# Seven Strassen products in place of the direct w1 and w3 products of a two-layer trunk, and w2 by groups of four blocks between them

## The chip, the core and the metric

One core of one Trainium2 chip runs the whole program in one launch. The metric is device time in microseconds, the median of several executions. The core has five engines: TensorE (PE; its weight loads are listed apart as PEld), VectorE (DVE), ScalarE (ACT), GpSimd (POOL) and SyncE (SP), which here issues the DMAs. Each works through a queue of its own in order and waits on semaphores for the others.

## The reference, cut to what matters

A sequence of 512 tokens with 1024 features goes through two layers. Each has a mixer (layer 0 sparse attention and pooling, layer 1 stick-breaking attention) and then a gated feed-forward part; both add to the residual x. All is float32, and the hidden width of the feed-forward part is 2816, that is 22 blocks of 128.

```python
def swiglu(h, w1, w3, w2):
    return (jax.nn.silu(h @ w1) * (h @ w3)) @ w2

for layer in range(DEPTH):
    ...
    h = rms_norm(x, norm_ffn_g[layer])
    x = x + swiglu(h, ffn_w1[layer], ffn_w3[layer], ffn_w2[layer])
```

## The kernel before, in words

The residual stands transposed: eight tiles xs of 128 features by 512 tokens. Every product of two float32 matrices is made of three passes: each operand is split into a high part, rounded to float32r, and the low rest, and TensorE adds high x high, high x low and low x high into one PSUM bank (`prods`, lines 204 to 206). A weight piece of 128x1024 is loaded by SP into a `raw` tile (three buffers), ScalarE writes the high part wh (`copy`, line 176), VectorE subtracts to get the low part wl (`split`, line 187). There are three pairs of wh and wl.

`Norm.chunk(c)` makes the two parts hh and hl of x times gain for one chunk of features (lines 253, 254) and adds its square to acc (264, 265). The factor of the norm, rb, comes from acc later (`stats`, `bcast`) and is multiplied in after the product.

`ffn(layer, nrm, nxt)` first loops over the 22 blocks f. For each it loads and splits the piece of w1 and of w3 and does 24 matmuls of 128x512 for each (8 chunks of features, three passes). Then it takes a = p1*rb on VectorE (308), silu on ScalarE (310), s*rb on GpSimd (311), a = p3*s on VectorE (312), and splits a into gh and gl (317 on ScalarE, 318 on VectorE). After all 22 blocks a second loop runs over the eight output chunks n: three pieces of w2, 66 matmuls of 128x512 into one bank, one addition to x (331), and then either the next layer's `chunk(n)` or the store to out.

The program is put to a scheduler in the order of the code. It assigns buffers and writes one fixed order for each engine. The mixers are written as steps in two tables, EVEN_ORDER and ODD_ORDER; their last steps, `oa` and `x` with first argument 1, are the output projections, which end with `nxt.chunk(n)`, so that the feed-forward part begins while they run.

## Time and profile before

| what | value |
|---|---|
| median of 3 runs | 1203.85 us (1203.02 to 1203.98) |
| span of the profiled execution, first to last instruction | 1202.7 us |
| TensorE busy | 1177.3 us, 98% |
| VectorE, ScalarE, GpSimd busy | 621.2, 481.0, 294.2 us |
| mean granted TensorE clock | 0.993 |
| DMA | 102.36 MB, mean 85 GB/s |

The page gives the profiled execution by its span alone; the median of the runs is 1.15 us longer. Matmuls are pipelined: the time of one in a row (some 0.39 us for 128x512) is its way through the array, and what a matmul costs in a stream is the distance from its start to the next one's. By the timeline, the even mixer lasts to 202.7 us, layer 0's w1/w3 loop to 444.0 us, its w2 loop to some 565 us, then the odd mixer to some 838 us, layer 1's w1/w3 loop to 1077.4 us and its w2 loop to the end.

### The profile page before, as it was taken

What the parts mean: (1) busy time and instruction counts of PE and PEld (TensorE: products, weight loads), DVE (VectorE), ACT (ScalarE), POOL (GpSimd) and SP (SyncE); (2) the same over time, 40 slices, a digit from 0 to 9 for tenths busy, and PEclk for the clock granted to TensorE, in tenths of its full rate; (3) what the DMA queues carried; (4) which work ended last, traced back from release to release, by engine and by line L of the source; (5) the groups of instructions that cost most, each with busy time, mean ns of one, the idle gap of its engine ahead of it and who ended that gap; (6) DMA issues with size and microseconds to landing.
All of it is one profiled execution on the core that took longest, in us unless ns stands there. A gap on an engine that the chain in (4) does not pass through costs nothing. (4 is left out here: it accounts for less than half of the span.)

```text
span 1202.7 us, 13889 instructions
## 1 busy us (share of the span) xinstructions
PE 1177.3 (98%) x5415; PEld 967.4 (80%) x5416; DVE 621.2 (52%) x851; ACT 481.0 (40%) x704; POOL 294.2 (24%) x324
## 2 busy tenths in 40 slices
PE   6999999999999999999999999999999999999998
PEld 3886758888888888888888888888888888888887
DVE  7499956434443433333457878867444434432221
ACT  4354564322223222223248778865323232321110
POOL 5246644111111110001023445433211111110000
PEclk8999999999999999999999999999999999999999
DMA  5222102232323223333221111112323233333330
GB/s 186 83 70 75 40 32 70 88 105 90 104 90 103 91 93 97 97 96 105 88 88 53 53 36 53 54 53 70 105 90 103 90 103 95 99 96 114 112 112 22
DMA packets 30737, 102.36 MB, mean 85 GB/s; under 512 B 3792, under 2 KB 4304, under 8 KB 30672
## 3 DMA queue, kind: packets, MB, share of 16 engines
q1 hardware_dynamic: 30240, 101.46, 26.4%
q8 instruction: 42, 0.69, 0.2%
q14 instruction: 23, 0.19, 0.1%
q10 hardware_dynamic: 432, 0.02, 0.0%
HBM read 99.37 MB, written 2.10 MB: 84 GB/s over the span
## 5 line engine op out<-in xcount | busy, mean ns | idle before, releaser
L205 PE MATMUL psum<-hl,wh_ffn_w 128*128 128x512 f32 x704 | 274.0, 389 | 0.3 <-DVE hl L254 0.3
L206 PE MATMUL psum<-hh,wl_ffn_w 128*128 128x512 f32 x704 | 274.1, 389 | 0.0
L204 PE MATMUL psum<-hh,wh_ffn_w 128*128 128x512 f32 x704 | 273.7, 389 | 0.0
L176 ACT ACTIVATE wh_ffn_w<-raw_ffn_w 128x1024 fp32r<-128x1024 f32 x88 | 93.4, 1061 | 305.4 <-PE psum L205 305.4
L311 POOL TENSOR_TENSOR s<-s,rb 128x512 f32<-128x512 f32 x44 | 76.8, 1748 | 378.3 <-ACT s L310 378.3
L205 PEld LDWEIGHTS psum<-hl,wh_ffn_w 128*128 128x128 f32 x704 | 132.2, 188 | 28.3 <-DVE hl L254 0.7
L206 PEld LDWEIGHTS psum<-hh,wl_ffn_w 128*128 128x128 f32 x704 | 132.2, 188 | 27.5
L204 PEld LDWEIGHTS psum<-hh,wh_ffn_w 128*128 128x128 f32 x704 | 132.2, 188 | 27.0
L204 PE MATMUL psum<-gh,wh_ffn_w 128*128 128x512 f32 x352 | 138.7, 394 | 0.0
L206 PE MATMUL psum<-gh,wl_ffn_w 128*128 128x512 f32 x352 | 138.0, 392 | 0.0
L205 PE MATMUL psum<-gl,wh_ffn_w 128*128 128x512 f32 x352 | 136.6, 388 | 0.0
L187 DVE TENSOR_TENSOR wl_ffn_w<-raw_ffn_w,wh_ffn_w 128x1024 fp32r<-128x1024 f32 x88 | 109.2, 1240 | 23.2 <-ACT wh_ffn_w L176 22.8
L176 ACT ACTIVATE wh_ffn_w<-raw_w 128x1024 fp32r<-128x1024 f32 (+1 forms) x48 | 47.5, 990 | 183.3 <-PE psum L205 158.5
L187 DVE TENSOR_TENSOR wl_ffn_w<-raw_w,wh_ffn_w 128x1024 fp32r<-128x1024 f32 (+1 forms) x48 | 54.6, 1137 | 122.4 <-ACT wh_ffn_w L176 122.4
L312 DVE TENSOR_TENSOR a<-psum,s 128x512 f32<-128x512 f32 x44 | 30.4, 691 | 138.2 <-PE psum L206 134.7
L308 DVE TENSOR_TENSOR a<-psum,rb 128x512 f32<-128x512 f32 x44 | 30.4, 692 | 107.4 <-PE psum L206 107.3
L206 PEld LDWEIGHTS psum<-gh,wl_ffn_w 128*128 128x128 f32 x352 | 66.1, 188 | 15.5
L205 PEld LDWEIGHTS psum<-gl,wh_ffn_w 128*128 128x128 f32 x352 | 66.1, 188 | 14.8
L204 PEld LDWEIGHTS psum<-gh,wh_ffn_w 128*128 128x128 f32 x352 | 66.2, 188 | 13.2
L265 POOL TENSOR_TENSOR acc<-acc,sq 128x512 f32<-128x512 f32 x28 | 42.0, 1501 | 140.4 <-ACT sq L264 139.7
L254 DVE SCALAR_TENSOR_TENSOR hl<-x,gain_t,hh 128x512 fp32r<-128x512 f32 x32 | 42.0, 1329 | 4.0 <-ACT hh L253 4.0
L204 PE MATMUL psum<-hh,wh_q 128*128 128x512 f32 x96 | 39.0, 406 | 1.8 <-DVE wh_q L178 1.8
(293 smaller groups left out, 2083.2 us busy)
## 6 DMA issues: line engine op xcount, KB each, us to landing
raw_ffn_w<-in_w_dram SPq DMA_DIRECT2D x88, 512.0 KB, 3.5
raw_w<-in_w_dram SPq DMA_DIRECT2D x32, 512.0 KB, 3.5
raw_w<-in_w_dram SPq DMA_DIRECT2D x16, 384.0 KB, 3.1
raw_v<-in_w_v_dram SPq DMA_DIRECT2D x8, 512.0 KB, 3.6
raw_q<-in_w_qk_dram SPq DMA_DIRECT2D x8, 512.0 KB, 3.5
raw_k<-in_w_qk_dram SPq DMA_DIRECT2D x8, 512.0 KB, 3.5
raw_o<-in_w_o_dram SPq DMA_DIRECT2D x8, 512.0 KB, 3.5
x<-in_x_dram SPq DMA_DIRECT2D x8, 256.0 KB, 5.3
```

The lines of the kernel that those rows point to most:

```text
L176: ac.activation(dst, src, AF.Copy, scale=scale)
L187: (ve if lo_eng == "dve" else gp).tensor_sub(lo[:, :cols], raw[:, :cols], f32(hi[:, :cols]))
L204: te.matmul(ps, wh, ah, start=(first and i == 0), stop=False)
L205: te.matmul(ps, wh, al, start=False, stop=False)
L206: te.matmul(ps, wl, ah, start=False, stop=(last and i == n - 1))
L254: ve.scalar_tensor_tensor(lo, xt, g, f32(hi), op0=ALU.mult, op1=ALU.subtract)
L265: gp.tensor_add(self.acc, self.acc, sq)
L308: ve.tensor_mul(a, p1, nrm.rb)
L311: gp.tensor_mul(s, s, nrm.rb)
L312: ve.tensor_mul(a, p3, s)
```

## The change

The first pair of blocks (f = 0, 1 in the old numbering) keeps the direct products (`Plain`, 24 matmuls of 128x512 for each of its four pieces), ordered by chunk of features. From the second pair on, ten pairs for each layer, each pair of blocks of w1 and likewise of w3 becomes a `Job`: the pair's weights are a two by two arrangement (block of the pair by even or odd chunk of features), and the activations are one too (even or odd chunk by half of the tokens). Seven products replace eight. Each is 12 matmuls of 128x256 (four pairs of chunks, three passes), so a Job has 84 of these where 48 of 128x512 stood. Products 1, 6, 7 and 4 add up in one bank A, 5 and 3 in a bank C, and 2 is alone in B. Between them ScalarE copies bank A out (u after product 1, u after 6, v after 7), and the next product adds to the same bank. VectorE puts the halves together (`put`).

Added work: for each layer `sums` makes the four sums T1 to T4 of the activations (8 copies on ScalarE, 16 operations of 128x256 on GpSimd, and four splits). For each Job GpSimd makes four sums of weights (128x512, lines 475 to 478 of the new kernel), and ScalarE and VectorE split the raw first block, the two tiles of sums s12 and s34 (128x1024 each) and the block a22 (128x512).

w2 is done by `Down(q, m)`: four blocks of the hidden dimension (the last group has two) times two output chunks, 24 matmuls of 128x512 into two banks, then two additions to x. One stands after each Job from the third pair on; the rest stand at the end. The number of w2 matmuls is the same, 528 for each layer; additions to x in this part rise from 16 to 88 in all.

Memory moves as well: the pools of a mixer and of the norm's tiles are closed before its output projection, so that the tiles of the feed-forward part can be opened there; its first pieces are loaded during steps 4 and 6 of that projection. The feed-forward part has four raw buffers and five pairs of wh and wl.

```diff
-    def ffn(layer, nrm, nxt):
-        with tc.tile_pool(name=f"ffn{layer}", bufs=1) as fp:
-            gs = []
-            for f in range(NF):
-                wa = weights(w13[layer, f, 0], f"ffn_w1_{layer}_{f}")
-                wb = weights(w13[layer, f, 1], f"ffn_w3_{layer}_{f}")
-                p1 = take()
-                dense(p1, wa, nrm.h)
-                if f == 0:
-                    nrm.stats()
...
-            for n in range(KC):
-                ps = take((n,))
-                pairs = []
-                for k0 in range(0, NF, 8):
...
-                    pairs += [(wcol(w, k - k0), gs[k]) for k in range(k0, k1)]
-                prods(ps, pairs)
-                ve.tensor_add(xs[n], xs[n], ps)
...
+        def sums(self, i, pool):
+            b = pool.tile([P, 4, HT], F32, name=f"b{self.idx}_{i}", tag="s12")
+            t = pool.tile([P, 4, HT], F32, name=f"t{self.idx}_{i}", tag="s34")
+            for e in range(2):
+                c = 2 * i + e
+                dst = b[:, 2 * e : 2 * e + 2, :].rearrange("p a b -> p (a b)")
+                ac.activation(dst, xs[c], AF.Copy, scale=gain_t[:, self.idx, c : c + 1])
+            gp.tensor_sub(t[:, 0, :], b[:, B12, :], b[:, B11, :])
+            gp.tensor_sub(t[:, 1, :], b[:, B22, :], t[:, 0, :])
+            gp.tensor_sub(t[:, 2, :], b[:, B22, :], b[:, B12, :])
+            gp.tensor_sub(t[:, 3, :], b[:, B21, :], t[:, 1, :])
+            hi, lo = self.pairs[i]
+            ac.copy(hi[:, 4:8, :], t)
+            ve.tensor_sub(lo[:, 4:8, :], t, f32(hi[:, 4:8, :]))
...
+            self.nraw += 1
+            return (self.fr if self.nraw % 4 == 1 else rawp).tile([P, D], F32, name=name, tag="raw")
...
+            self.nsplit += 1
+            p = self.fw if self.nsplit % 5 in (1, 2) else wsp
+            return [p.tile([P, D], F32R, name=f"w{x}_{name}", tag=f"w{x}") for x in "hl"]
...
+        def gated(f, i):
+            q, r = divmod(f, 2)
+            if (f, i) == (2 * q, 1) or q not in gsplit:
+                if q not in gsplit:
+                    p = (big, stage.more)[q % 2]
+                    gsplit[q] = [p.tile([P, 4, T], F32R, name=f"gs{x}_{layer}_{q}", tag=f"o{x}") for x in "hl"]
+            h, l = [t[:, 2 * r + i, :] for t in gsplit[q]]
+            src = values[f][i]
+            ac.copy(h, src)
...
+                gp.tensor_add(z[0], a21, a22)
+                gp.tensor_sub(z[1], z[0], a11)
+                gp.tensor_sub(z[2], a11, a21)
+                gp.tensor_sub(z[3], a12, z[1])
+                wa = split_into(stage.two(f"a{name}"), raw[0])
+                w12 = split_into(stage.two(f"s{name}"), s12)
+                w34 = split_into(stage.two(f"t{name}"), s34)
+                h = stage.fr.tile([P, n, P], F32R, name=f"wh_b{name}", tag="wbh")
+                l = stage.fr.tile([P, n, P], F32R, name=f"wl_b{name}", tag="wbl")
+                ac.copy(h, a22)
+                ve.tensor_sub(l, a22, f32(h))
...
+            BANK = {1: "A", 6: "A", 7: "A", 4: "A", 2: "B", 5: "C", 3: "C"}
+            RHS = {1: B11, 2: B21, 3: B22, 4: T4, 5: T1, 6: T2, 7: T3}
+            def prod(self, p):
+                b = self.BANK[p]
+                first = b not in self.open
+                if first:
+                    self.open[b] = take()
+                ps = self.open[b][:, :HT]
+                r = self.RHS[p]
+                for k in range(KC // 2):
+                    wh, wl = self.wt[p](k)
+                    ah, al = (x[:, r, :] for x in nrm.pairs[k])
+                    te.matmul(ps, wh, ah, start=first, stop=False, skip_group_check=True)
+                    te.matmul(ps, wh, al, start=False, stop=False, skip_group_check=True)
+                    te.matmul(ps, wl, ah, start=False, stop=(k == KC // 2 - 1), skip_group_check=True)
+                    first = False
+                nm = f"{self.w}_{layer}_{self.f}"
+                if p == 1:
+                    self.u = stage.fg.tile([P, T], F32, name=f"u{nm}", tag="u")
+                    ac.copy(self.u[:, LAT], ps)
+                elif p == 6:
+                    ac.copy(self.u[:, ERL], ps)
+                elif p == 7:
+                    self.u3 = stage.fr.tile([P, HT], F32, name=f"v{nm}", tag="u3")
+                    ac.copy(self.u3, ps)
+                    self.put(1, ERL, self.u3, "C")
+                elif p == 2:
+                    self.put(0, LAT, self.u[:, LAT], "B")
+                    give(self.open["B"])
+                elif p == 4:
+                    self.put(1, LAT, None, "A")
+                    give(self.open["A"])
+                elif p == 3:
+                    self.put(0, ERL, self.u[:, ERL], "C")
+                    give(self.open["C"])
+            def put(self, i, half, a, b):
+                ps = self.open[b][:, :HT]
+                last = (i, half) in ((1, LAT), (0, ERL))
+                c = gate_tile(self.f)[i]
+                d = c if self.w == 0 else value_tile(self.f)[i]
+                if a is not None:
+                    ve.tensor_add(d[:, half], ps, a)
+                if self.w:
+                    if a is None:
+                        ve.tensor_mul(d[:, half], ps, c[:, half])
+                    elif i == 1:
+                        ve.tensor_mul(d[:, half], d[:, half], c[:, half])
+                    elif last:
+                        ve.tensor_mul(d, d, c)
+                    if last:
+                        gated(self.f, i)
+                elif a is None:
+                    ve.tensor_mul(d[:, half], ps, rb(half))
+                    ve.tensor_mul(d[:, ERL], d[:, ERL], rb(ERL))
+                elif last:
+                    ve.tensor_mul(d, d, nrm.rb)
+                if last and self.w == 0:
+                    ac.activation(d, d, AF.Silu)
+                    gp.tensor_mul(d, d, nrm.rb)
...
+        class Down:
...
+                self.ps = [take(), take()] if ps is None else ps
+                for i in range(2):
+                    g = [tuple(t[:, j, :] for t in gsplit[q]) for j in range(nb)]
+                    prods(self.ps[i], [(col(w, i * nb + j), g[j]) for j in range(nb)], ps is None, last)
+                if not last:
+                    return
+                for i in range(2):
+                    n = 2 * m + i
+                    ve.tensor_add(xs[n], xs[n], self.ps[i])
+                    give(self.ps[i])
...
+        start = [Plain(0, 0)]
+        yield
+        start.append(Plain(0, 1))
+        yield
+        for k in range(KC):
+            for p in start:
+                p.prod(k)
+        nrm.stats()
+        nrm.bcast()
+        for p in start:
+            p.done()
+        for i in range(KC // 2):
+            nrm.sums(i, stage.fs)
+        y = None
+        for f in range(1, NP):
+            for w in range(2):
+                x = Job(f, w)
+                for who, p in ((x, 1), (x, 2), (y, 4), (x, 6), (y, 3), (x, 5), (x, 7)):
+                    if who is not None:
+                        who.prod(p)
+                y = x
+                q, r = divmod(f, 2)
+                if q:
+                    Down(q - 1, 2 * r + w)
+        y.prod(4)
+        y.prod(3)
+        nrm.close()
+        if nxt is not None:
+            nxt.open()
+        q = NF // 4
+        d = Down(q - 1, 2, last=False)
+        Down(q, 0)
+        Down(q, 1)
+        Down(q, 2, d.ps)
+        d = Down(q - 1, 3, last=False)
+        Down(q, 3, d.ps)
...
+                if (name, *args) == ("x", 1, 0):
+                    es_wk.close()
+                    nrm.close()
+                    nxt.open()
+                    after.open()
```

Three places show how the rows of an engine's order change. The last number of a name is that of the tile.

TensorE, layer 1, between blocks 20 and 21 before (hh3 and hl3 are the parts of the normed residual, wh and wl those of the weights):

```order
L205 MATMUL psum_76<-hl3_6_6547,wh_ffn_w3_1_20_8000 128x512
L206 MATMUL psum_76<-hh3_6_6546,wl_ffn_w3_1_20_8001 128x512
L204 MATMUL psum_76<-hh3_7_6566,wh_ffn_w3_1_20_8000 128x512
L205 MATMUL psum_76<-hl3_7_6567,wh_ffn_w3_1_20_8000 128x512
L206 MATMUL psum_76<-hh3_7_6566,wl_ffn_w3_1_20_8001 128x512
L204 MATMUL psum_76<-hh3_0_6377,wh_ffn_w1_1_21_8064 128x512
```

and now at the start of the Job of w1 for pair 6 (wh_a0_1_6 is the split of its first block, gsh and gsl the split gated values, wh_w2_1_1_3 the w2 piece of group 1, chunks 6 and 7):

```order
L511 MATMUL psum_70<-hh3_0_7656,wl_a0_1_6_9554 128x256
L509 MATMUL psum_70<-hh3_1_7718,wh_a0_1_6_9553 128x256
L510 MATMUL psum_70<-hl3_1_7719,wh_a0_1_6_9553 128x256
L204 MATMUL psum_70<-gsh_1_1_8647,wh_w2_1_1_3_9513 128x512
L205 MATMUL psum_70<-gsl_1_1_8648,wh_w2_1_1_3_9513 128x512
L204 MATMUL psum_70<-gsh_1_1_8647,wh_w2_1_1_3_9513 128x512
L205 MATMUL psum_70<-gsl_1_1_8648,wh_w2_1_1_3_9513 128x512
L511 MATMUL psum_70<-hh3_1_7718,wl_a0_1_6_9554 128x256
L509 MATMUL psum_70<-hh3_2_7780,wh_a0_1_6_9553 128x256
L510 MATMUL psum_70<-hl3_2_7781,wh_a0_1_6_9553 128x256
```

Products of half the width replace the direct ones, and the w2 products stand among them.

VectorE, layer 1, blocks 18 to 20 before (wl is the low part of a weight piece, gl that of the gated value):

```order
L308 TENSOR_TENSOR a_1_18_7912<-psum_76,rb3_6650 128x512
L187 TENSOR_TENSOR wl_ffn_w3_1_19_7931<-raw_ffn_w3_1_19_7928,wh_ffn_w3_1_19_7930 128x1024
L312 TENSOR_TENSOR a_1_18_7912<-psum_76,s_1_18_7914 128x512
L187 TENSOR_TENSOR wl_ffn_w1_1_20_7995<-raw_ffn_w1_1_20_7992,wh_ffn_w1_1_20_7994 128x1024
L318 TENSOR_TENSOR gl_1_18_7919<-a_1_18_7912,gh_1_18_7918 128x512
L308 TENSOR_TENSOR a_1_19_7982<-psum_76,rb3_6650 128x512
L187 TENSOR_TENSOR wl_ffn_w3_1_20_8001<-raw_ffn_w3_1_20_7998,wh_ffn_w3_1_20_8000 128x1024
L312 TENSOR_TENSOR a_1_19_7982<-psum_76,s_1_19_7984 128x512
```

and now around the Job of w1 for pair 6 (u and v are copies of bank A, c the gate, g the value, s12 and s34 the sums of weights):

```order
L394 TENSOR_TENSOR wl_w2_1_2_0_9673<-raw_w2_1_2_0_9669,wh_w2_1_2_0_9672 128x1024
L541 TENSOR_TENSOR c0_1_6_9595<-psum_70,u0_1_6_9581 128x256
L394 TENSOR_TENSOR wl_s1_1_6_9717<-s12_1_1_6_9706,wh_s1_1_6_9716 128x1024
L545 TENSOR_TENSOR g1_1_5_9435<-psum_70,c1_1_5_9274 128x256
L485 TENSOR_TENSOR wl_b0_1_6_9566<-raw_w0_1_6_1_9545,wh_b0_1_6_9565 128x512
L420 TENSOR_TENSOR gsl_1_2_9290<-g1_1_5_9435,gsh_1_2_9289 128x512
L541 TENSOR_TENSOR g0_1_5_9434<-psum_70,u1_1_5_9420 128x256
L549 TENSOR_TENSOR g0_1_5_9434<-g0_1_5_9434,c0_1_5_9273 128x512
L394 TENSOR_TENSOR wl_a1_1_6_9713<-raw_w1_1_6_0_9702,wh_a1_1_6_9712 128x1024
L394 TENSOR_TENSOR wl_t1_1_6_9721<-s34_1_1_6_9707,wh_t1_1_6_9720 128x1024
L420 TENSOR_TENSOR gsl_1_2_9290<-g0_1_5_9434,gsh_1_2_9289 128x512
L541 TENSOR_TENSOR c1_1_6_9596<-psum_70,v0_1_6_9666 128x256
```

Low parts of weights, of sums and of gated values and the putting together of products now stand between any two additions to x.

GpSimd, layer 1, where before only line-311 products of 128x512 stood, one for each block; now, around pair 7 (s12 and s34 of w3 for pair 6, then of w1 for pair 7, then the gates of pair 6):

```order
L476 TENSOR_TENSOR s12_1_1_6_9706<-s12_1_1_6_9706,raw_w1_1_6_0_9702 128x512
L477 TENSOR_TENSOR s34_1_1_6_9707<-raw_w1_1_6_0_9702,raw_w1_1_6_1_9704 128x512
L478 TENSOR_TENSOR s34_1_1_6_9707<-raw_w1_1_6_0_9702,s12_1_1_6_9706 128x512
L475 TENSOR_TENSOR s12_0_1_7_9867<-raw_w0_1_7_1_9865 128x512
L477 TENSOR_TENSOR s34_0_1_7_9868<-raw_w0_1_7_0_9863,raw_w0_1_7_1_9865 128x512
L476 TENSOR_TENSOR s12_0_1_7_9867<-s12_0_1_7_9867,raw_w0_1_7_0_9863 128x512
L478 TENSOR_TENSOR s34_0_1_7_9868<-raw_w0_1_7_0_9863,s12_0_1_7_9867 128x512
L559 TENSOR_TENSOR c1_1_6_9596<-c1_1_6_9596,rb3_7976 128x512
L559 TENSOR_TENSOR c0_1_6_9595<-c0_1_6_9595,rb3_7976 128x512
```

Ten operations of 128x512 stand here for each pair of blocks, in place of two.

## Rows read from the trace of the kernel before

**Rows 1.** Part 1 of the page: busy us (share) xinstructions of each engine
```profile
PE 1177.3 (98%) x5415; PEld 967.4 (80%) x5416; DVE 621.2 (52%) x851; ACT 481.0 (40%) x704; POOL 294.2 (24%) x324
```

**Rows 2.** Part 4 of the page: the chain that ended last, by line
```profile
PE psum L204 10%; PE psum L206 10%; PE psum L205 10%; PE psum L282 0%; PE psum L271 0%; DVE x L331 0%
```

**Rows 3.** Timeline, TensorE, w1/w3 loop: start us, us, engine, line, operation
```profile
299.82 0.39 PE L204 MATMUL psum<-hh,wh_ffn_w 128*128 128x512 f32 x1
...
319.55 0.39 PE L204 MATMUL psum<-hh,wh_ffn_w 128*128 128x512 f32 x1
```

**Rows 4.** The same view in the w2 loop of layer 1
```profile
1149.96 0.39 PE L204 MATMUL psum<-gh,wh_ffn_w 128*128 128x512 f32 x1
...
1169.87 0.39 PE L204 MATMUL psum<-gh,wh_ffn_w 128*128 128x512 f32 x1
```

**Rows 5.** The same view, the 256-wide stretch of the even mixer
```profile
44.73 0.28 PE L472 MATMUL psum<-wl_nat,hh 128*128 128x256 f32 x1
...
50.24 0.28 PE L473 MATMUL psum<-wh_nat,hl 128*128 128x256 f32 x1
```

**Rows 6.** Windows: busy us (count) by engine; granted clock; DMA share, GB/s
```profile
44.70:50.40 5.70, 5.70 (x49) 5.67 (x48) 3.19 (x4) 5.55 (x24) 0.00 (x0) 1.00 0.29 95
...
240.00:430.00 190.00, 190.00 (x840) 157.34 (x839) 77.53 (x88) 55.83 (x70) 31.12 (x18) 1.00 0.30 97
```

**Rows 7.** Timeline of all engines at the end of the span
```profile
1198.48 0.40 PE L206 MATMUL psum<-gh,wl_ffn_w 128*128 128x512 f32 x1
...
1198.92 0.69 DVE L331 TENSOR_TENSOR x<-x,psum 128x512 f32<-128x512 f32 x1 [13.50 <-PE psum L206]
...
1199.63 0.34 SPq L336 DMA_DIRECT2D out_dram<-x  x1
```

**Rows 8.** Groups by line and form: busy us, mean ns | idle before
```profile
L187 DVE TENSOR_TENSOR wl_ffn_w<-raw_ffn_w,wh_ffn_w 128x1024 fp32r<-128x1024 f32 x88 | 109.2, 1240 | 23.2 <-ACT wh_ffn_w L176 22.8 <-issue 0.2
...
L176 ACT ACTIVATE wh_ffn_w<-raw_ffn_w 128x1024 fp32r<-128x1024 f32 x88 | 93.4, 1061 | 305.4 <-PE psum L205 305.4
...
L308 DVE TENSOR_TENSOR a<-psum,rb 128x512 f32<-128x512 f32 x44 | 30.4, 692 | 107.4 <-PE psum L206 107.3
...
L317 ACT CAST gh<-a 128x512 fp32r<-128x512 f32 x44 | 27.3, 621 | 4.3 <-DVE a L312 4.0
...
L310 ACT ACTIVATE s<-a 128x512 f32<-128x512 f32 x44 | 27.4, 628 | 0.0
...
L436 ACT ACTIVATE rl<-psum 128x256 f32<-128x256 f32 x4 | 1.5, 381 | 2.4 <-DVE kzl L509 1.5 <-PE psum L434 0.8
...
L205 PEld LDWEIGHTS psum<-hl,wh_ffn_w 128*128 128x128 f32 x704 | 132.2, 188 | 28.3 <-DVE hl L254 0.7
```

**Rows 9.** Timeline of VectorE and GpSimd at the end of the even mixer
```profile
195.06 1.41 POOL L265 TENSOR_TENSOR acc<-acc,sq 128x512 f32<-128x512 f32 x1 [0.84 <-ACT sq L264]
...
195.23 1.78 DVE L254 SCALAR_TENSOR_TENSOR hl<-x,gain_t,hh 128x512 fp32r<-128x512 f32 x1
...
198.40 0.75 DVE L254 SCALAR_TENSOR_TENSOR hl<-x,gain_t,hh 128x512 fp32r<-128x512 f32 x1 [0.79 <-ACT hh L253]
```

**Rows 10.** The same view in the w1/w3 loop of layer 1
```profile
857.83 2.54 POOL L311 TENSOR_TENSOR s<-s,rb 128x512 f32<-128x512 f32 x2 [8.95 <-ACT s L310]
...
866.80 1.23 DVE L187 TENSOR_TENSOR wl_ffn_w<-raw_ffn_w,wh_ffn_w 128x1024 fp32r<-128x1024 f32 x1 [0.23 <-ACT wh_ffn_w L176]
...
867.38 1.79 POOL L311 TENSOR_TENSOR s<-s,rb 128x512 f32<-128x512 f32 x1 [7.01 <-ACT s L310]
```

**Rows 11.** Waits: who waited <- released by: us, times, longest
```profile
ACT pr L565 <- POOL mx L563: 21.4, 11, 7.4
```

**Rows 12.** Timeline of TensorE where widths alternate, odd mixer
```profile
664.62 0.22 PE L215 MATMUL psum<-shB,nall_r 128*128 128x128 f32 x1
...
666.24 0.63 PE L215 MATMUL psum<-shA,ntri_r 128*128 128x512 f32 x2
```

More of the change, by code (lines that the diff above doesn't have):

```diff
@@ new lines, in tile_trunk, with __init__, pool, open_more @@
+    class Ffn:
+        def __init__(self, layer, nrm, nxt):
+            self.layer, self.nrm, self.nxt = layer, nrm, nxt
+            self.es = ExitStack()
+        def pool(self, name, bufs):
+            return self.es.enter_context(tc.tile_pool(name=f"{name}{self.layer}", bufs=bufs, reuse_waits="tile"))
+        def open_more(self):
+            self.more = self.pool("fm", 1)
+        def open(self):
+            self.nraw, self.nsplit = 0, 0
+            self.fr = self.pool("fr", 1)
+            self.fw = self.pool("fw", 2)
+            self.fs = self.pool("fs", 1)
+            self.fg = self.pool("fg", 2)
+            self.steps = ffn(self)
+        def first(self):
+            next(self.steps)
+        def run(self):
+            for _ in self.steps:
+                pass
+            self.es.close()
+        def raw(self, name):
+            self.nraw += 1
+            return (self.fr if self.nraw % 4 == 1 else rawp).tile([P, D], F32, name=name, tag="raw")
+        def two(self, name):
+            self.nsplit += 1
+            p = self.fw if self.nsplit % 5 in (1, 2) else wsp
+            return [p.tile([P, D], F32R, name=f"w{x}_{name}", tag=f"w{x}") for x in "hl"]
@@ L342, in even @@
+    def even(nrm, nxt, w_first, after):
+        with ExitStack() as es_wk:
+            ap = es_wk.enter_context(tc.tile_pool(name="ev", bufs=1, reuse_waits="tile"))
+            wk = es_wk.enter_context(tc.tile_pool(name="evw", bufs=2, reuse_waits="tile"))
             OWN = [slice(0, 64), slice(64, 128)]
+            identb = ap.tile([P, P], BF16, name="identb")
+            ve.tensor_copy(identb, ident)
             one = ap.tile([P, 1], F32, name="one")
@@ L650, in step_oa @@
             def step_oa(n):
-                if n % 2 == 0:
-                    S["oa", n // 2] = weights(w_o0[4 + n // 2], f"oa_{n // 2}")
+                for i in {0: (0,), 2: (1,), 4: (2, 3)}.get(n, ()):
+                    S["oa", i] = weights(w_o0[4 + i], f"oa_{i}")
+                if n in (4, 6):
+                    after.first()
                 ps = take(EVEN_BANKS["oa"])
@@ L758, in step_k @@
                     S["k", c, j] = t
-            oh = [ap.tile([P, T], F32R, name=f"o1h{c}") for c in range(KC)]
-            ol = [ap.tile([P, T], F32R, name=f"o1l{c}") for c in range(KC)]
+            o1 = [[p.tile([P, 4, T], F32R, name=f"o1{x}{i}", tag=f"o{x}") for i, p in enumerate((big, after.more))] for x in "hl"]
+            oh, ol = [[o[c // 4][:, c % 4, :] for c in range(KC)] for o in o1]
             PLACE = {0: ("A", 0), 1: ("B", 0), 2: ("C", 0), 3: ("B", 384)}
@@ L866, in step_x @@
             def step_x(h, n):
-                if n % 2 == 0:
-                    S["x", h, n // 2] = weights(w_o1[4 * h + n // 2], f"o1_{h}_{n // 2}")
+                for i in {0: (0,), 2: (1,), 4: (2, 3) if h else (2,), 6: () if h else (3,)}.get(n, ()):
+                    S["x", h, i] = weights(w_o1[4 * h + i], f"o1_{h}_{i}")
+                if h and n in (4, 6):
+                    after.first()
                 ps = take(ODD_BANKS["x"] if h == 0 else (ODD_BANKS["y"][n],))
@@ L877, in odd @@
             for name, *args in ODD_ORDER:
+                if (name, *args) == ("x", 1, 0):
+                    es_wk.close()
+                    nrm.close()
+                    nxt.open()
+                    after.open()
                 steps["step_" + name](*args)
@@ L884, in load_x @@
         nc.sync.dma_start(xs[c], x[c * P : (c + 1) * P, :])
-    norms = [Norm(i) for i in range(4)]
-    raw = wraw.tile([P, D], F32, name="raw_qi_0", tag="raw")
-    w_first = wsp.tile([P, D], F32R, name="wh_qi_0", tag="wh"), wsp.tile([P, D], F32R, name="wl_qi_0", tag="wl")
+    norms = [Norm(0), PairNorm(1), Norm(2), PairNorm(3)]
+    norms[0].open()
+    raw = rawp.tile([P, D], F32, name="raw_qi_0", tag="raw")
+    w_first = [wsp.tile([P, D], F32R, name=f"w{x}_qi_0", tag=f"w{x}") for x in "hl"]
     halves = [slice(0, T), slice(T, D)]
@@ L904, in tile_trunk @@
         norms[0].squared(c)
-    even(norms[0], norms[1], w_first)
-    ffn(0, norms[1], norms[2])
+    ffns = Ffn(0, norms[1], norms[2]), Ffn(1, norms[3], None)
+    even(norms[0], norms[1], w_first, ffns[0])
+    ffns[0].run()
     load_exp_ln()
-    odd(norms[2], norms[3])
-    ffn(1, norms[3], None)
+    odd(norms[2], norms[3], ffns[1])
+    ffns[1].run()
 def _station(w):
```

176 lines of the change are left out of this document (131 added, 45 removed).

## The prediction

> **What bounds the kernel now.** I read the page's totals first: TensorE is busy 98% of the span, VectorE 52%, ScalarE and GpSimd less [rows 1]. The chain that ended last follows PSUM from matmul to matmul, 10% on each of the three lines of `prods` and hardly anything elsewhere [rows 2]. A stretch inside layer 0's w1/w3 loop confirms it: 840 matmuls fill 190.00 us without a gap while the others are busy 78 us or less, at a granted clock of 1.00 [rows 6]. So a matmul saved there is time saved, until another engine keeps TensorE waiting.
>
> What one matmul costs is the distance between starts. In the w1/w3 loop two starts lie 87 intervals apart: 19.73/87 = 0.2268 us for 128x512 [rows 3]; in the w2 loop 19.91/87 = 0.2289 us [rows 4]. For 128x256 the even mixer has a stretch: 5.51 us over 46 intervals = 0.1198 us [rows 5].
>
> All sums below go against the span, 1202.7 us; the median is 1.15 us above it, and I add that at the end.
>
> **TensorE.** Each layer has ten Strassen pairs with two Jobs each, 40 Jobs in all. Out go 40 x 48 = 1920 matmuls, 1920 x 0.2268 = 435.4 us. In come 40 x 84 = 3360 at 0.1198 us, 402.5 us. That is -32.9 us, not the eighth that seven products for eight suggest, since half a width costs 0.528 of a whole one. The first pair (direct) and the 1056 w2 matmuls keep number and width: nothing. The gain is gone at 435.4/3360 = 0.1296 us per matmul.
>
> I take 0.1198, because in that stretch each matmul also had its own weights: 49 matmuls, 48 loads, loads 99% busy, no gap [rows 6]. A load listed at 0.188 us in the 512-wide loop [rows 8] is therefore hidden or shorter. The Trainium skill ("TensorE: Matmul & The Clock Gate", Part 3: Packing small matmuls) says that a load overlaps running matmuls only if it targets other row groups; its section on LDWEIGHTS gives about P/1.2 ns, 107 ns for 128 columns. By that rule 1440 more loads would add an estimated 154 us; the stretch contradicts the rule, as 0.1198 us leaves no room for load and matmul in turn.
>
> **The other engines in a steady pair** (from the third pair on, 18 in both layers). TensorE needs 168 x 0.1198 + 48 x 0.2289 = 31.1 us. VectorE: eight low parts of 128x1024 (three for each Job, one for each Down), 8 x 1.24 [rows 8]; a22, gated values and additions to x, eight of 128x512 at 0.69 (the price of L308 [rows 8] and L331 [rows 7]); ten 128x256 operations, at about 0.41 by the line through 0.69 and 1.24, my estimate; the two full-width multiplies 2 x 0.69. Sum 9.9 + 5.5 + 4.1 + 1.4 = 20.9 us. ScalarE: 8 x 1.06 + 2 x 0.62 + 6 copies of bank x 0.38 + 2 silu x 0.63 + 2 casts x 0.62 = 14.5 us [rows 8]. GpSimd: ten operations of 1.27 us (two took 2.54), 12.7 us [rows 10]. Each alone fits into 31.1 us.
>
> What they do to one another is the open cost. Beside VectorE's hl (1.78 us, against 0.75 alone) GpSimd's acc ran [rows 9]; a GpSimd product that started inside VectorE's wl took 1.79 instead of 1.27 us, ending some 1.14 us after wl did [rows 10]. So operations of the two that read only SBUF take turns. Such work is 14.9 us on VectorE (the low parts, a22, gated parts and full-width multiplies; not what reads PSUM) and 12.7 us on GpSimd, 27.6 of the 31.1 us. It fits, with little room. The first Strassen pair of a layer has no Down: TensorE 20.1 us, turns 12.4 + 12.7 = 25.1 us, 5 us too much, to be paid from work done ahead in the first pair, or by waiting.
>
> *What waits for them.* (1) After product 1, ScalarE must copy bank A before product 6 adds to it; between stand 24 matmuls, 2.9 us, against 0.38 us plus what is ahead in its queue. The same holds after 6 (product 5 hides it, 12 matmuls with product 3's 12). ScalarE's order is fixed, and one item in it that waits for GpSimd holds all behind it: in the odd mixer such a wait came 11 times, 21.4 us, the longest 7.4 [rows 11]. (2) Casting s12 and s34 stands behind GpSimd's four sums, on that same queue. (3) A Down that needs the pair just finished has an add, a multiply, a cast and a low part ahead, 0.41 + 0.69 + 0.62 + 0.69 = 2.4 us, against about 2.9 us of matmuls between. Covers of 3 us over chains of 2 to 3 us mean occasional misses. Bounds for a steady pair: 0 (all hidden), and 2.5 us (VectorE's 20.9 plus every GpSimd operation in series, 33.6, less 31.1). A gain below 0 is excluded, since no matmul in the rows runs faster than 0.1198. I take 0.3 us, near the lower bound since 88% is under 100% and the buffers (five split pairs for three) let work run ahead: 18 x 0.3 = 5.4 us.
>
> *Start of each feed-forward part.* From the output projection to the end of the second pair TensorE has 2 x 96 matmuls of 128x512 and 168 half ones, 43.8 + 20.1 = 64 us. The work in turns there is eight normed chunks, 8 x (0.75 + 1.41) = 17.3 us [rows 9], the sixteen operations for T1 to T4 at half of 1.27, 10.2, eight low parts (four direct pieces, four for T1 to T4), 9.9, the first pair's gating, 2 x 1.27 + 2 x 0.69 = 3.9, and the second pair's 25.1: 66 us, and T1 to T4 can be made only after the last chunk. Bounds 0 and 8 us (5 us too much in pair 2, plus 3 for what comes late here); I take 3 for each layer, 6 in all.
>
> *At nothing:* the moved pools and the mixers' order (the covered matmuls are those of before; uncovered, a late first piece costs one load, up to 3 us); 48 more DMAs on SP, at 0.34 us of issue each [rows 7], same bytes, DMA at 30% and 97 GB/s in the loop [rows 6]; the end, where two additions to x follow the last matmuls instead of one, the first behind the second chunk's (one more 0.69 us if uncovered [rows 7]); the extra additions to x, in VectorE's sum above, for which only a bank is waited for.
>
> **Sum:** 1202.7 - 32.9 + 5.4 + 6 = 1181.2 us of span, some **1182.5 us** as a median.
>
> **Rivals.**
> *No new waits (0.03):* 1202.7 - 32.9 + 1.15 = 1171 us. For it: each engine fits alone. Against: at 88% of turns, with 2 to 3 us of cover, it would need luck.
> *Turn-taking costs most of the gain (0.20):* 0.7 to 1.6 us for each steady pair and 4 to 5 at each start, so 13 to 29 + 8 to 10 us, 1192 to 1205 us. For it: both VectorE and GpSimd were seen to stretch [rows 9, 10]. Against: the PSUM-reading share of VectorE can run beside GpSimd. The Trainium skill ("SBUF — State Buffer", SBUF: two separate sides) calls the shared port pair an exclusive lock for the whole instruction, which a VectorE operation with two SBUF inputs takes against GpSimd; the rows agree (1.78 for 0.75, 1.79 for 1.27).
> *VectorE becomes the bound, slower (0.12):* if each GpSimd operation holds VectorE up in full, a steady pair takes 33.6 us, 18 x 2.5 = 45 us, and the two first Strassen pairs 15.7 + 12.7 = 28.4 instead of 20.1, 17 us more: 1171 + 62 = 1233 us. The place is the split of s12 and s34 ahead of products 6, 5, 7 and 3. It decides from 1.7 us a pair on, where 32.9 is used up. Against: it needs GpSimd to meet SBUF-only VectorE work every time, and such work is only half of a pair's time.
> *Half width costs more here (0.03):* where 128, 256 and 384 wide matmuls alternate in the odd mixer (mean 256), a step was 1.62/12 = 0.135 us [rows 12]. 3360 x 0.135 = 453.6 us, +18.2 us in place of -32.9, with the waits 1234 us. Against: Jobs are uniform like the stretch of [rows 5], only at Down's edges do widths alternate.
> *Loads not hidden (0.02):* at 0.188 us a matmul [rows 8], 631.7 us, about 1400 us. Against: [rows 6].
> *The change does less than it says:* excluded by the order, in which the half-width products stand on TensorE; no chance given.
>
> **How the numbers follow.** The forecast (some waits) has 0.60, 1172 to 1192 us by the bounds above. It, no waits and most of the turn-taking rival make up 8 in 10 and more: range **1171 to 1205 us**, which leaves out the two slow ends. Under 0.2% (2.4 us) a measurement of this kernel tells nothing from no change: same is 1201.4 to 1206.3. Faster 0.60 + 0.03 + 0.17 = 0.80; same 0.04 (the turn-taking rival's end, and a little of the slow one); slower 0.16 (VectorE-bound 0.11, 0.05 of width and loads).
>
> **What would show it.** Starts of L509 to L511 0.120 us apart and the weight loads near 99% in Jobs: TensorE's term. TensorE's idle time ahead of L509 to L511 and L204, by releaser: below 1 us a pair, most of it behind ScalarE's copies and splits. L394 on VectorE with a mean of 1.3 to 1.5 instead of 1.24, L475 to L478 on GpSimd nearer 1.75 than 1.27. A gap at the first Job of each layer. The granted clock stays at 1.00 in the Jobs; if waits broke the stream and it fell towards the lower level, every matmul after a wait would cost more, and the forecast be wrong at once. It would also be wrong if L394 reached 2 us, or the step in Jobs 0.13.

## The result, and the profile after

The changed kernel takes 1182.37 us (median of 4 runs, 1181.45 to 1183.79) against 1203.91 us (1203.02 to 1204.01): a ratio of 0.9826, 95% interval 0.9812 to 0.9840, 21.5 us less. The forecast was 1182.5. That it is right to 0.2 us is luck in part: two terms of the sum were wrong by some 10 us each, in opposite directions, and the runs show where.

Part 1 of the page after (compare [rows 1]), and the chain that ended last, by line (compare [rows 2]):

```profile
PE 1142.0 (97%) x6855; PEld 1000.8 (85%) x6856; DVE 857.5 (73%) x1171; ACT 603.5 (51%) x928; POOL 559.3 (47%) x516
...
PE psum L509 5%; PE psum L511 5%; PE psum L510 5%; PE psum L206 3%; PE psum L204 3%; PE psum L205 3%; DVE x L581 0%; ACT v L522 0%
```

TensorE is still the bound, with the half-width lines in the chain now. VectorE went from 52 to 73%, GpSimd from 24 to 47%. The end of the span is as before: 4.2 us from the last matmul's start in both profiles.

The timeline of TensorE in a steady pair of layer 0, product 1 and those after it (compare [rows 3, 5]):

```profile
464.01 0.28 PE L509 MATMUL psum<-hh,wh_a 128*128 128x256 f32 x1
...
474.28 0.28 PE L510 MATMUL psum<-hl,wh_a 128*128 128x256 f32 x1
```

Between these two starts lie 88 intervals: 10.27/88 = 0.1167 us, not the 0.1198 of the even mixer. 3360 x 0.1167 = 392.1 us stand where 435.4 stood: -43.3 us. The direct products of the first pair, which go to four banks in turn, three matmuls to each, came at 0.2333 us in place of 0.2268 (188 steps): 192 x 0.0066 = 1.3 us back. So the matmul term is -42.0 us.

How much of it arrived, from the first direct w1 matmul to the last w2 matmul of each layer, start to start in the timeline: layer 0 took 361.9 us and takes 350.3, layer 1 367.0 and 358.6. That is 11.7 + 8.4 = 20.1 us. **21.9 us were lost again**: 9.3 in layer 0, 12.6 in layer 1. (The profiled spans, 1202.7 and 1179.5, differ by 23.2: the even mixer, whose order has not changed, ended 3.4 us earlier in this execution, at 199.3 us. In the profiles of the kernels below it ends anywhere from 198.4 to 201.5 us, always earlier than in the one profile of before. Some 0.6 us of the 3.4 is the faster step of its output projection, told in the last section; how much of the rest is a difference between executions stays open.)

TensorE's waits after, costliest first (who waited <- released by: us, times, longest):

```profile
PE psum L509 <- DVE ms L283: 7.0, 2, 4.0
...
PE psum L509 <- DVE rb L300: 2.0, 1, 2.0
...
PE psum L204 <- ACT wh_w L393: 1.8, 1, 1.8
```

With smaller ones of 0.2 to 1.3 us, the feed-forward parts hold 14.3 us of listed waits. In the timeline all of them lie between 228 and 263 us and between 851 and 878 us, that is in the first two Strassen pairs of each layer. Then nothing, as the windows over the steady pairs show (busy us (count) of PE, PEld, DVE, ACT, POOL; granted clock; DMA):

```profile
270.00:540.00 270.00, 270.00 (x1873) 251.16 (x1873) 191.59 (x244) 118.35 (x172) 116.70 (x80) 1.00 0.34 104
890.00:1140.00 250.00, 250.00 (x1763) 233.61 (x1763) 184.75 (x233) 113.14 (x164) 117.38 (x80) 1.00 0.33 103
```

520 us without a gap. A pair takes 216 matmuls. In the timeline six pairs running, from 313.83 to 497.40 us, take 183.57 us, 30.6 us each, where 31.1 were forecast; the cheaper half-width step accounts for it (168 x 0.0031 = 0.5). The first of the two windows gives more for each matmul, as it ends among the last w2 groups, which are all of full width.

The first and largest wait, in the timeline of all engines at the start of layer 0's first Job:

```profile
223.53 1.23 DVE L394 TENSOR_TENSOR wl_s<-s,wh_s 128x1024 fp32r<-128x1024 f32 x1 [2.25 <-ACT wh_s L393]
...
223.62 2.27 POOL L478 TENSOR_TENSOR s<-raw_w,s 128x512 f32<-128x512 f32 x1
...
225.92 1.04 ACT L393 CAST wh_t<-s 128x1024 fp32r<-128x1024 f32 x1 [2.43 <-POOL s L478]
...
227.00 1.32 DVE L394 TENSOR_TENSOR wl_t<-s,wh_t 128x1024 fp32r<-128x1024 f32 x1 [2.25 <-ACT wh_t L393]
...
227.82 0.36 ACT L517 COPY u<-psum 128x256 f32<-128x256 f32 x1
228.24 0.15 DVE L283 TENSOR_SCALAR ms<-psum 128x4 f32<-128x4 f32 x1
```

GpSimd's sum waits its turn behind VectorE's low part (2.27 us, ending 1.13 after wl_s), ScalarE's cast waits for the sum, the copy of bank A stands behind two casts in ScalarE's queue, and the norm's ms, whose matmuls were through at 222.7, stands behind wl_t on VectorE. TensorE goes on at 228.54. The Trainium skill ("SBUF — State Buffer", SBUF: two separate sides) has a loser of the shared port pair wait out the whole instruction; the rows of wl_s and of GpSimd's sum agree.

Why a product should wait for ms, which it doesn't read, the kernel tells (`take` and `give`): there are eight PSUM banks. The first pair holds four until its gating, which needs rb; products 1 and 2 of the first Job have two more, the statistics one, and the broadcast of rb the last. So product 5, which is next in TensorE's order, gets its bank when VectorE has read ms out of it, and product 1 of the second Job gets one when rb has been copied out, which is the wait for rb in the list above. No run gave the start other banks.

A wait costs more than its length. TensorE after that wait:

```profile
229.48 0.41 PE L509 MATMUL psum<-hh,wh_s 128*128 128x256 f32 x1
...
232.25 0.41 PE L510 MATMUL psum<-hl,wh_s 128*128 128x256 f32 x1
```

13 intervals in 2.77 us, 0.213 instead of 0.117 us. The windows show the granted clock there and after two later waits:

```profile
228.54:232.50 3.96, 3.96 (x21) 3.96 (x22) 0.98 (x1) 0.00 (x0) 3.96 (x3) 0.57 0.11 43
851.50:855.90 4.40, 3.08 (x13) 2.81 (x14) 2.15 (x2) 1.19 (x2) 4.40 (x4) 0.50 0.42 128
878.30:881.10 2.80, 2.80 (x14) 2.71 (x14) 2.80 (x4) 0.37 (x1) 2.80 (x2) 0.51 0.55 172
```

0.50 is the lower level, 1.2 GHz; the first window begins 0.6 us before the clock fell. 39 steps at 0.21 us cost 39 x 0.095 = 3.7 us. With the 14.3 us of waits, and 0.1 to 0.3 us at the first steps behind each wait, that accounts for most of the 21.9 us.

The operations that take turns (by form, of the whole kernel; compare L187 in [rows 8] and [rows 10]):

```profile
L478 POOL TENSOR_TENSOR s<-raw_w,s 128x512 f32<-128x512 f32 x40 | 68.1, 1703 | 2.3
...
L394 DVE TENSOR_TENSOR wl_a<-raw_w,wh_a 128x1024 fp32r<-128x1024 f32 x40 | 64.2, 1606 | 4.8 <-ACT wh_a L393 4.8
...
L394 DVE TENSOR_TENSOR wl_w<-raw_w,wh_w 128x1024 fp32r<-128x1024 f32 x40 | 57.1, 1427 | 2.6 <-ACT wh_w L393 2.6
...
L475 POOL TENSOR_TENSOR s<-raw_w 128x512 f32<-128x512 f32 x40 | 55.4, 1384 | 163.4 <-DMA raw_w<-in_w_dram 151.0 <-DVE gsl L420 7.3 <-DVE wl_s L394 3.6
```

All low parts of L394 in the Jobs and groups have a mean of 1.43 us (1.24 before), the four sums 1.50 (1.27 alone). Both engines stretch, and in the steady pairs TensorE doesn't wait for it.

### The profile page after: what moved, and what is told of

It is laid out like the page before. It is cut to its first block, busy times and chain, and to the rows that moved or that the text cites. A ratio compares the mean times of both kernels' runs of the same rounds, so it can differ in the third digit from the quotient of the medians.

```text
span 1179.5 us, 17799 instructions
## 1 busy us (share of the span) xinstructions
PE 1142.0 (97%) x6855; PEld 1000.8 (85%) x6856; DVE 857.5 (73%) x1171; ACT 603.5 (51%) x928; POOL 559.3 (47%) x516
## 5 line engine op out<-in xcount | busy, mean ns | idle before, releaser
L205 PE MATMUL psum<-gsl,wh_w 128*128 128x512 f32 x352 | 137.6, 391 | 0.0
L204 PE MATMUL psum<-gsh,wh_w 128*128 128x512 f32 x352 | 135.3, 392 | 1.8 <-ACT wh_w L393 1.8
L206 PE MATMUL psum<-gsh,wl_w 128*128 128x512 f32 x352 | 135.5, 391 | 0.0
L475 POOL TENSOR_TENSOR s<-raw_w 128x512 f32<-128x512 f32 x40 | 55.4, 1384 | 163.4 <-DMA raw_w<-in_w_dram 151.0
L509 PE MATMUL psum<-hh,wh_s 128*128 128x256 f32 x320 | 91.0, 284 | 7.8 <-DVE ms L283 7.0
L511 PE MATMUL psum<-hh,wl_s 128*128 128x256 f32 x320 | 90.8, 284 | 1.3 <-DVE wl_s L394 1.3
L509 PE MATMUL psum<-hh,wh_a 128*128 128x256 f32 x320 | 89.4, 280 | 2.0 <-DVE rb L300 2.0
L510 PE MATMUL psum<-hl,wh_s 128*128 128x256 f32 x320 | 90.6, 283 | 0.0
L509 PE MATMUL psum<-hh,wh_t 128*128 128x256 f32 x320 | 89.5, 280 | 0.4 <-DVE c L541 0.4
L510 PE MATMUL psum<-hl,wh_t 128*128 128x256 f32 x320 | 89.2, 279 | 0.0
L511 PE MATMUL psum<-hh,wl_t 128*128 128x256 f32 x320 | 89.2, 279 | 0.0
L204 PEld LDWEIGHTS psum<-gsh,wh_w 128*128 128x128 f32 x352 | 65.8, 188 | 13.9 <-ACT wh_w L393 2.0
L205 PEld LDWEIGHTS psum<-gsl,wh_w 128*128 128x128 f32 x352 | 66.1, 188 | 12.3
L478 POOL TENSOR_TENSOR s<-raw_w,s 128x512 f32<-128x512 f32 x40 | 68.1, 1703 | 2.3
```

The lines of the kernel that those rows point to most:

```text
L204: te.matmul(ps, wh, ah, start=(first and i == 0), stop=False)
L205: te.matmul(ps, wh, al, start=False, stop=False)
L206: te.matmul(ps, wl, ah, start=False, stop=(last and i == n - 1))
L475: gp.tensor_add(z[0], a21, a22)
L478: gp.tensor_sub(z[3], a12, z[1])
L509: te.matmul(ps, wh, ah, start=first, stop=False, skip_group_check=True)
```

## The experiments

The theory after this reading: the loss lies at the start of each feed-forward part alone, in GpSimd's queue and in what stands behind it. The rival: turn-taking costs something in every pair. Times in this section are medians; the changed kernel's 1182.4 is the measure, ratios are to the kernel before, timed anew with each set of runs. Its medians lie between 1202.1 and 1203.9, so of a difference between two sets up to 2 us says little; the times of the feed-forward parts are of one profile each.

**e1**, T1 to T4 by VectorE:

```diff
-            gp.tensor_sub(t[:, 0, :], b[:, B12, :], b[:, B11, :])
+            ve.tensor_sub(t[:, 0, :], b[:, B12, :], b[:, B11, :])
...
```

> The sixteen operations for T1 to T4 of each layer are made by VectorE instead of GpSimd; all else as in the changed kernel (its 1182.4 us is the measure). Theory: the time that is lost (some 18 us against 38.6 us of saved matmul time) is lost at the start of the two feed-forward parts, in GpSimd's queue. There GpSimd is relieved of 16 x 0.74 = 11.8 us a layer, VectorE, mostly idle there, gets 16 x 0.41 = 6.6 us; the waits ahead of the first Jobs (6.0 and 8.3 us, and the half-clock matmuls behind them) fall to less than half: 1170 to 1177 us, 1174 likeliest. Rival: the loss lies in the taking of turns in the steady pairs; then the time stays within 0.2%, 1180 to 1185 us.

Measured: 1177.37 us, ratio 0.9786 (0.9773 to 0.9800), 5.0 us faster than the change. The feed-forward parts, as above, take 347.6 and 356.3 us: 2.7 and 2.3 less. So the start does hold lost time, but the gain is short of the likeliest 8 us (the time is 0.4 us over the theory's range), and the waits don't fall to less than half: TensorE's listed waits in the feed-forward parts are 11.1 us against 14.3. The largest:

```profile
PE psum L509 <- DVE ms L283: 5.1, 1, 5.1
...
PE psum L509 <- DVE rb L300: 3.5, 2, 2.9
```

In layer 1 GpSimd now stands for 10.9 us and starts the first Job's sums 27.7 us after the first direct matmul, only 2.4 earlier than in the changed kernel, when the last T sums let go of the one pair s12, s34. The amount of GpSimd's work was not all of it.

**e2**, no sums of weights from the fifth pair on:

```diff
-                gp.tensor_add(z[0], a21, a22)
...
+                if f < 4:
+                    gp.tensor_add(z[0], a21, a22)
...
-                w12 = split_into(stage.two(f"s{name}"), s12)
+                w12 = split_into(stage.two(f"s{name}"), s12 if f < 4 else raw[1])
```

> From the fifth pair on GpSimd's four sums of weights are left out and the raw pieces are split in their place (so those products are of other weights, with the same matmuls); casts, low parts and all else stay. Theory (the steady pairs hide their turns): no change, 1180 to 1184 us. Rival (turns between VectorE and GpSimd cost something in every pair): 5 to 16 us less, 1166 to 1177 us.

Measured: 1182.71 us, ratio 0.9830 (0.9814 to 0.9845). No change. The window that answers to the one above:

```profile
270.00:540.00 270.00, 270.00 (x1881) 251.55 (x1880) 180.02 (x246) 120.66 (x174) 40.45 (x25) 1.00 0.34 104
```

GpSimd has 40 instead of 117 us of work and VectorE 12 us less, and TensorE gets through 1881 matmuls instead of 1873, 0.4%, in a stretch whose mix of widths differs slightly. The casts of the late pairs no longer wait for sums either, so this run takes both away, and neither was worth anything. The rival of steady turn-taking falls.

**e3**, direct products for all pairs, w2 groups kept between them:

```diff
-                x = Job(f, w)
-                for who, p in ((x, 1), (x, 2), (y, 4), (x, 6), (y, 3), (x, 5), (x, 7)):
-                    if who is not None:
-                        who.prod(p)
-                y = x
+                x = Plain(f, w)
+                for k in range(KC):
+                    x.prod(k)
+                x.done()
```

> All pairs of blocks by direct products in the order of the first pair, without T1 to T4 and without Jobs, but with the new w2 groups between the pairs. Theory (all of the gain is the Jobs' matmuls, the w2 placement is worth nothing): 1182.4 + 38.6 - 16 us of start waits that go, and up to 13 us more if all direct matmuls go at the 0.2335 us of the changed kernel's first pair instead of 0.2268: 1203 to 1219 us. Rival: the groups of w2 between the pairs gain or cost something by themselves: under 1200, or over 1222 us.

Measured: 1214.45 us, ratio 1.0095 (1.0080 to 1.0111). The trace lists no wait of TensorE in either feed-forward part. In a steady stretch:

```profile
229.34 0.39 PE L205 MATMUL psum<-hl,wh 128*128 128x512 f32 x1
...
256.17 0.39 PE L206 MATMUL psum<-hh,wl 128*128 128x512 f32 x1
```

115 intervals, 0.2333 us. The two parts take 741.2 us against 728.9 before, 12.3 more; 2112 x 0.0066 = 13.9 us comes from the pace of the direct products alone. The w2 groups between the pairs are worth nothing measurable by themselves: the whole gain is the Jobs'. Why the direct products go at the slower pace here is open (last section).

**e4**, each weight sum made twice from the fifth pair on:

```diff
                 gp.tensor_sub(z[3], a12, z[1])
+                if f >= 4:
+                    gp.tensor_add(z[0], a21, a22)
+                    gp.tensor_sub(z[1], z[0], a11)
+                    gp.tensor_sub(z[2], a11, a21)
+                    gp.tensor_sub(z[3], a12, z[1])
```

> From the fifth pair on GpSimd makes each of its four sums twice, 14 pairs in both layers. Theory (VectorE's work on SBUF alone and GpSimd's take turns): 14.9 + 22.9 = 37.8 us of turns for 31 us of matmuls, 6 to 7 us more for each pair, 84 to 98 us in all: 1266 to 1280 us. Rival (the two only slow one another now and then): GpSimd's 22.9 us fit beside 31 us of matmuls, 1182 to 1200 us.

Measured: 1265.88 us, ratio 1.0520 (1.0505 to 1.0535), 83.5 us over the changed kernel, 6.0 for each of 14 pairs, 0.1 us under the range. The window and the largest wait:

```profile
300.00:580.00 280.00, 250.92 (x1647) 231.23 (x1646) 192.09 (x216) 101.34 (x152) 198.14 (x123) 0.95 0.29 89
```

```profile
ACT wh_s L393 <- POOL s L481: 144.2, 27, 7.9
```

1647/216 = 7.6 pairs at 14.9 us of VectorE's SBUF work and 123 GpSimd operations at 1.27 make 113 + 156 = 269 us of turns in 280, 96%; the changed kernel has 8.7 x 14.9 + 80 x 1.27 = 231 in 270, 86%. So the room that the forecast saw was real and of about that size. One thing stays open: the casts wait for sums that now take 10 us in one chain with a single pair s12, s34, so latency and exhausted turns are not told apart here.

The next runs were to find what holds the start. **e5** gives T1 to T4 tiles of their own, without more memory:

```diff
-            b = pool.tile([P, 4, HT], F32, name=f"b{self.idx}_{i}", tag="s12")
-            t = pool.tile([P, 4, HT], F32, name=f"t{self.idx}_{i}", tag="s34")
+            b = [pool.tile([P, T], F32, name=f"b{e}{self.idx}_{i}", tag=f"g{e}", bufs=1) for e in range(2)]
+            t = [pool.tile([P, T], F32, name=f"t{e}{self.idx}_{i}", tag="u") for e in range(2)]
...
-            nrm.sums(i, stage.fs)
+            nrm.sums(i, stage.fg)
```

> T1 to T4 are made in tiles that the start leaves unused (those of the values and of u) instead of s12 and s34; GpSimd makes them as in the changed kernel, in splits of 128x512. Theory after the first four runs: at the start of a feed-forward part a chain runs through the one pair s12, s34: copies, sums, cast, low part, four times, and only then may the first Job's sums be written there. With tiles of their own GpSimd's waits of 2.5 us between the T sums remain, but the first Job's sums fill them: 1174 to 1180 us against 1182.4. Rival (it is the amount of GpSimd's work that counts, 11.8 us of T sums and 10 of weight sums): 1181 to 1185 us.

Measured: 1219.68 us, ratio 1.0144 (1.0125 to 1.0163): 37 us slower than the change. Neither theory had that.

```profile
PE psum L512 <- ACT hh L344: 30.7, 8, 10.5
```

L344 is the cast of T1 to T4. In the program's order the first pair's gating claims the tiles g before the sums do, so T1 and T2 now waited for the gating, which waits for rb. So e5 doesn't test its theory, and neither do e8 and e9, which have the same order.

**e6**, the norm's statistics earlier:

```diff
         for k in range(KC):
+            if k == KC - 1:
+                nrm.stats()
             for p in start:
                 p.prod(k)
-        nrm.stats()
         nrm.bcast()
```

> The changed kernel with the norm's statistics (the four matmuls with ones, and ms) put ahead of the first pair's last chunk of products instead of behind it. Theory: the wait of the first Job for ms (3.0 and 4.0 us) comes from ms standing behind low parts on VectorE that wait for GpSimd, and the one for rb (2.0 us) from the power on GpSimd behind sums; both are then early: 1174 to 1180 us. Rival (the first Job needs its sums from GpSimd anyway, so that the wait only changes its name): 1181 to 1185 us.

Measured: 1179.01 us, ratio 0.9808 (0.9795 to 0.9821); the interval overlaps the changed kernel's. The median lies in the theory's range; by the ratios the gain is 2.2 us, and in the profile the feed-forward parts take 349.7 and 357.4 us, 1.7 less in all. The waits:

```profile
PE psum L509 <- ACT wh_s L393: 4.2, 2, 4.0
PE psum L292 <- POOL rcol L286: 4.0, 2, 2.7
...
PE psum L509 <- DVE c L541: 2.5, 1, 2.5
```

No wait for ms or rb is left, and most of the time is: the listed waits still come to 13.6 us, now for the cast of the sums and for the power on GpSimd. So the theory holds by its number and the rival by its mechanism, and a wait's name is the last of several that end close together.

**e8** (e1 and e5) and **e9** (e8 and e6):

> T1 to T4 by VectorE and in the tiles of their own: the runs e1 and e5 together. Theory: GpSimd can begin the first Job's sums as soon as their pieces have arrived, some 10 us earlier than in e1, and the waits ahead of the first Jobs nearly vanish: 1167 to 1173 us. Rival (VectorE becomes what is waited for, with 6.6 us more and its turns with GpSimd): no better than e1, 1175 to 1180 us.

> T1 to T4 by VectorE, in tiles of their own, and the norm's statistics ahead of the last chunk. Theory: of the 17 us that TensorE stood or went slow at the two starts 2 to 5 are left: 1164 to 1169 us. Rival (the starts have a floor that is set by casts and low parts, 8 us in each): 1172 to 1177 us.

Measured: 1209.54 us, ratio 1.0061 (1.0049 to 1.0074), and 1207.72 us, 1.0046 (1.0032 to 1.0059). Both inherit the fault of e5: TensorE's waits for L344 are 24.6 and 29.9 us.

**f5, f8 and f9** are e5, e8 and e9 with the sums ahead of the gating in the program, here as in f5 and f8; in f9 they stand further ahead, before the first pair's products:

```diff
+        for i in range(KC // 2):
+            nrm.sums(i, stage.fg)
         nrm.stats()
         nrm.bcast()
         for p in start:
             p.done()
-        for i in range(KC // 2):
-            nrm.sums(i, stage.fg)
```

> As e5, but the T sums stand ahead of the first pair's gating in the program, so that they get the tiles of values and u first (in e5 they got them only after the gating had used them, and the first Job waited 10 us for T2). GpSimd makes them as before. Theory (the one pair s12, s34 holds the first Job's sums back): 1172 to 1179 us. Rival (GpSimd's amount of work counts): 1180 to 1185 us.

> As f5, with T1 to T4 by VectorE; the norm's statistics as in the changed kernel. GpSimd can make the first Job's sums while the output projection runs. Theory: 1167 to 1174 us, the waits for ms and rb left (2 to 4 us in each layer). Rival (VectorE is what is waited for): as e1, 1175 to 1180 us.

> As f8, with the norm's statistics ahead of the first pair's last chunk too. Theory: TensorE stands for less than 3 us at the two starts together: 1162 to 1168 us. Rival (casts and low parts set a floor of some 8 us in each): 1172 to 1177 us.

Measured: f5 1181.11 us, 0.9818 (0.9805 to 0.9832); f8 1181.46 us, 0.9818 (0.9802 to 0.9834); f9 **1175.17 us**, 0.9775 (0.9758 to 0.9792). So tiles of their own do nothing while GpSimd makes the T sums (the rival of f5), f8 misses both of its expectations on the slow side and is 4.1 us slower than e1, which has the one pair of tiles. Only f9 gains, 7.2 us by its median; its theory had 1162 to 1168 us, and it lies in the rival's 1172 to 1177. Since f9 differs from f8 in two ways, the earlier statistics and the place of the sums, its gain isn't shown to be that of the statistics. It is the lowest time, 2.25% under the kernel before, but not clearly better than e1: the intervals overlap, the feed-forward parts take 703.1 us in f9 and 703.9 in e1, and the listed waits come to 11.7 and 11.1. What f9 waits for:

```profile
PE psum L206 <- DVE wl L397: 5.4, 2, 2.8
...
PE psum L512 <- DVE c L544: 5.0, 2, 2.5
```

```profile
225.66 1.05 ACT L396 CAST wh_s<-s 128x1024 fp32r<-128x1024 f32 x1 [6.11 <-PE psum L205]
```

VectorE, busy with T1 to T4, is late with the first pair's own low parts; and the cast of the first Job's sums waits 6.1 us for a split tile that the first pair's matmuls hold to their end.

**g1** takes both away: T1 to T4 by GpSimd as in f5, statistics early and the sums before the first pair's products as in f9, and the w1 pieces of the first pair finished before the w3 pieces:

```diff
+        for ks in (range(KC // 2), range(KC // 2, KC)):
...
+                for p in start:
+                    if p is start[1]:
+                        nrm.stats()
+                    for k in ks:
+                        p.prod(k)
```

> T1 to T4 by GpSimd in tiles of their own as in f5, the norm's statistics earlier, and the first pair's products so ordered that the w1 pieces are through with their second half of chunks before the w3 pieces begin it, which frees two of the five pairs of split tiles 5 us sooner (in f9 the cast of the first Job's sums waited for such a pair until the first pair's last matmul). Theory: what was left at the start in f9 was VectorE's load with T1 to T4 (2.9 and 2.6 us ahead of the first pair's own low parts) and the split tiles: 1168 to 1174 us. Rival (with GpSimd making T1 to T4 the sums for the second Job, and the power behind them, are late again): 1176 to 1182 us.

Measured: 1182.67 us, ratio 0.9824 (0.9809 to 0.9838). The rival.

```profile
PE psum L292 <- POOL rcol L286: 8.0, 2, 5.2
...
PE psum L281 <- POOL acc L275: 3.8, 1, 3.8
```

Every large wait now ends on GpSimd: the power and the norm's sum stand behind T sums and weight sums in its queue. g1's order of the products with T1 to T4 by VectorE was not tried.

## Why the prediction was right, and where it was right by luck

**Bound and direction: right.** TensorE's matmuls are the chain before and after, and a matmul saved was time saved in the steady pairs. e3 shows that the gain is the Jobs' alone.

**"I take 0.1198": too dear.** The Jobs go at 0.1167, so the term is -43.3 us instead of -32.9; with the first pair's slower direct products, which I costed at nothing, -42.0. The 46 steps of [rows 5] were a short stretch of another stage, whose own pace is not fixed: after the change it goes at 0.1183 (91 steps). That loads are hidden at half width was right. The sentence of the Trainium skill that the prediction goes by ("TensorE: Matmul & The Clock Gate", Part 3: Packing small matmuls), by which a load overlaps only with other row groups, is contradicted again: 0.1167 us a step with a load of its own for each matmul. The same part names a background weight buffer as a second way to load ahead, which these rows don't contradict.

**Steady pairs, 5.4 us: none.** From the third Strassen pair of each layer on no wait stands in the trace, and e2 gains nothing. The turns held (86%, 88 forecast), the lengthening of L394 to 1.43 us lay in the range given, and e4 shows how far the edge was: twice the sums, 6.0 us a pair. Two signs failed: L475 to L478 came to 1.50 us, not nearer to 1.75 than to 1.27, and TensorE's waits were mostly behind ms and rb, not behind ScalarE. The turn-taking rival put the loss in the wrong stage; at the start turns lengthen single steps (2.27 us for 1.27), but no run shows what they cost there. Its own sum was wrong as well: 1171 + 29 + 10 is 1210 us, not 1205. Nor do the bounds given, 0 to 2.5 us a pair and 0 to 8 a start, make 1172 to 1192 us; they make 1171 to 1232.

**Start of each feed-forward part, 3 us a layer, bounds 0 and 8: the step that failed.** It cost 9.3 and 12.6 us, over the upper bound in both layers. I compared two totals, 66 us of turns with 64 us of matmuls. What the rows show instead is order: T sums go through one pair of tiles, in turn with casts and low parts; the first Job's sums come after them in GpSimd's queue; ms and the power stand behind these on VectorE and GpSimd; the copy of bank A stands behind casts that wait for GpSimd, as the prediction had it for the Jobs under (1) and (2); and two products wait for the banks of ms and rb, which the prediction didn't count. T sums off GpSimd's queue took 5.0 us of it back in e1, so that much is shown; f5 shows that tiles of their own alone are worth nothing, and e6 and g1 that one wait taken away uncovers the next, GpSimd's in g1. For the rest of the 21.9 us, some 15 to 17 us, the cause is argued from the rows, not shown by a run; fewer banks held by the first pair would be the next thing to try.

**"The granted clock stays at 1.00 in the Jobs": wrong for some 11 us** behind the longer waits, at a cost of 3.7 us. The prediction named it as a danger, and left it out of the bounds.

So 32.9 - 11.4 = 21.5 us was forecast (by its own terms 1182.35, given as some 1182.5), and 42.0 - 21.9 = 20.1 us is what the feed-forward parts show. What the prediction put at nothing held: the end of the span, the DMAs (104 GB/s, no wait of TensorE for a load in the feed-forward parts) and the mixers' order.

## What to carry to other kernels

Take the pace of a new instruction from the longest clean stretch that has it, and give a short one from another stage its own range: 3% of 3360 matmuls was 10 us here. Compare engines' totals for a steady loop, but for a start or an end write out each queue in its order, with the tiles and banks that pass from step to step. When a wait is taken away, look first at what else ended within a microsecond of it.

## What was not expected of the hardware

After some waits TensorE ran at its lower level for 3 to 4 us: after it had stood 2.96 us, the granted clock of the next stretch was 0.57, after 4.02 us 0.50, and after 1.75 us, up to 876.20, it had fallen by 878.30 (0.51). After 1.96 us at 236 us it did not fall (121 matmuls in a row at 0.1167). So the length of the wait alone doesn't decide it here.

Direct 128x512 matmuls come at two paces: 0.2268 us [rows 3] where one bank is added to, and 0.2333 in the first pair and all through e3, where banks change after every three. But the even mixer's output projection, in the same order, went at 0.2333 before and 0.2267 after (89 steps in each). So the order of banks does not explain it; the places of tiles in memory have changed there. The 256-wide stretch of that mixer went from 0.1198 to 0.1183 us as well (91 steps in each). The cause was not tried and stays open; for 2112 matmuls it is 14 us.
